# The end of a ReLU row-sum kernel: GpSimd alone waits for the stores and clears the semaphores

## Chip, cores and metric

The kernel runs on one core of one Trainium2 chip. The metric is device microseconds of one execution. Times in traces are microseconds from the start of the span, which is the first of the program's own instructions (SyncE's first load); ns are marked.

## The reference

```python
x = randn(32, 512, 1024)  # float32, 64 MiB
out = np.sum(np.maximum(x, 0), axis=-1)  # 32 x 512, float32
```

16,384 rows of 1,024 numbers are clamped at zero and summed. The data are read once, and the output is 64 KB.

## The kernel before

The body is written by hand with its own semaphores. Its last part and the closing block are what matters here. Three stores, all issued by SyncE, each add 16 to a semaphore `stored`; the last one writes two columns of the result, 1 KB.

```python
def tile_relu_sum_kernel(tc, x, out):
    nc = tc.nc
    sems = Semaphores(tc)
    tc.close()
    tc.compile()
    nc.cur_bb = nc.bb_map[tc.start_bb_name]
    body = nc.cur_bb.bb.instructions
    ends = list(body)
    body.clear()
    n_stores = relu_sum(nc, sems, x, out)
    body.extend(ends)

    nc.cur_bb = nc.bb_map[tc.start_bb_name + "_end"]   # the closing block
    body = nc.cur_bb.bb.instructions
    ends = list(body)
    body.clear()
    nc.sync.wait_ge(sems.stored, 16 * n_stores)
    body.extend(ends)
    issue_ahead_of_the_barrier(tc, EARLY)
# ... cut ...
    def store(m, n, act, dve):
        nonlocal n_store
        dst, src = sums(m, n)
        nc.sync.wait_ge(sems.act, act)
        nc.sync.dma_start(out=dst, in_=src).wait_op(sems.dve, dve, "sem-ge").then_inc(
            sems.stored, 16
        )
        n_store += 1
# ... cut: loads, clamps, sums ...
    store(NT - 2, 2, n_act, n_dve)
    return n_store
```

The closing block (`ends`) that the framework makes holds, in this order: a drain on SyncE; a barrier of all five engines; on GpSimd a drain and one instruction that clears the range of the kernel's semaphores; a second barrier of all engines. A barrier is a drain that adds to a gather semaphore and a wait for a release semaphore on four engines, and on GpSimd a drain, a wait for four arrivals and a release. (A drain names no tile in the trace; here it carries a wait for a semaphore or an increment of one, or neither. A release is the increment that lets the waiting engines go on.)

Of the kernel before, what the change touches and what calls it, by code (L numbers as in the profile page):

```python
# [23 lines left out]
def kernel(tc: tile.TileContext, x: bass.AP, out: bass.AP):  # L24
# [9 lines that stand above are left out]
    n_stores = relu_sum(nc, sems, x, out)  # L34
    body.extend(ends)

    nc.cur_bb = nc.bb_map[tc.start_bb_name + "_end"]
    body = nc.cur_bb.bb.instructions
    ends = list(body)
    body.clear()  # L40
    nc.sync.wait_ge(sems.stored, 16 * n_stores)
    body.extend(ends)
    issue_ahead_of_the_barrier(tc, EARLY)


# [169 lines left out]
    return n_store  # L215


def issue_ahead_of_the_barrier(tc: tile.TileContext, n_loads: int):


    SP = mybir.EngineType.SP
    blocks = tc.nc.main_func.blocks
    opening = blocks[0].instructions
    body = next(b for b in blocks if b.name == tc.start_bb_name).instructions
    loads = [i for i in body if i.engine == SP][:n_loads]
    for i in loads:
        assert isinstance(i, mybir.InstDMACopy)
        body.remove(i)
    at = next(
        n  # L230
        for n, i in enumerate(opening)
        if i.engine == SP and isinstance(i, mybir.InstDrain)
    )
    opening[at:at] = loads
# [30 lines left out]
```

## Time and profile before

| | before |
|---|---|
| time, median | 163.16 us (163.13 to 163.45, 3 runs) |
| span of the program's own instructions | 160.70 us |
| share of the DMA engines' span taken by loads and stores | 97.6% |
| VectorE, ScalarE busy | 73%, 64% |
| last increment of `stored` | 159.90 us |
| time minus span | 2.44 us |

From the page of the kernel before, the span, the busy times (microseconds, share of the span, instructions) and the DMA queue (packets, megabytes, share of 16 engines' span):

```profile
span 160.7 us, 162 instructions
...
DVE 117.0 (73%) x47; ACT 102.8 (64%) x52; POOL 0.2 (0%) x4
...
q1 hardware_dynamic: 2592, 67.18, 97.6%
```

The body is bound by reading HBM: the transfers fill 97.6% of the queue's span and the two compute engines wait for them. The end of the chain that ended last (start, length, what):

```profile
127.97 28.83 DMA piece<-in_x_dram
156.80 0.02 issue
156.82 1.20 DVE piece L136 x6
158.02 0.02 issue
158.04 0.44 DVE piece L204
158.48 0.01 DVEq L29
```

So arithmetic is over at 158.48 us, and 2.2 us of the span follow it. What SyncE waits for there (total, times, longest):

```profile
SPq L29 <- DMA out_dram<-res: 1.1, 1, 1.1
...
SPq L29 <- PEq L29: 0.6, 2, 0.4
```

Line 29 is that of all instructions that the framework made. They are listed in the view of that source line (durations least, median, most in ns; first and last start in us):

```profile
L29 POOLq EVENT_SEMAPHORE  x4: 17/17/17, 160.0 to 160.6; - x4
L29 POOLq DRAIN  x3: 34/41/82, 0.7 to 160.4; - x3
L29 SPq DRAIN  x3: 7/7/7, 159.9 to 160.2; - x3
L29 PEldq DRAIN  x2: 8/8/8, 0.9 to 160.3; - x2
L29 ACTq DRAIN  x2: 14/596/1177, 156.5 to 160.2; - x2
L29 DVEq DRAIN  x2: 19/236/452, 158.1 to 160.2; - x2
L29 SPq EVENT_SEMAPHORE  x2: 17/17/17, 160.1 to 160.6; - x2
L29 ACTq EVENT_SEMAPHORE  x2: 17/17/17, 160.1 to 160.6; - x2
L29 DVEq EVENT_SEMAPHORE  x2: 21/21/21, 160.1 to 160.6; - x2
L29 PEldq EVENT_SEMAPHORE  x2: 51/51/51, 160.1 to 160.7; - x2
L29 POOLq EVENT_SEMAPHORE_RANGE_CLEAR  x1: 136/136/136, 160.3 to 160.3; - x1
```

These are SyncE's wait, the two barriers and the clearing between them. Some first drains start early (TensorE's at 0.9 us, ScalarE's at 156.5), as these engines have nothing left to do; everything after the start of SyncE's waiting drain at 159.92 runs in the last 0.8 us. None of it counts as busy time, so the page's busy rows show nothing of this.

The program's span is not the end of the timed interval. Time minus span is 2.44 us, and the trace's semaphore events show what happens in it. These events stand in the trace itself, and no view of the profile prints them. Semaphore 2, which no instruction of the program names, is incremented nine times (I call this a walk, the time between two increments a hop, and the engine whose turn it is a station); semaphores 7 to 255 are updated, the last of them from 161.36 to 162.02 us, from the middle of this walk on; then comes a second walk of nine. I call this stretch the runtime's ending. That name, "sync-barrier semaphore" for semaphore 2 and "resets" for the updates are names only: the trace tells neither who makes these events nor what the updates write. A walk of the same nine increments stands ahead of the span, too: the eight hops of this opening walk took 371 ns.

| event, kernel before | us |
|---|---|
| last increment of `stored` | 159.901 |
| walk 1, increments 1, 2, 3 | 160.936, 160.970, 161.175 |
| walk 1, increment 9 | 161.460 |
| walk 2, increments 1, 2 | 162.248, 162.358 |
| walk 2, increment 9 | 162.682 |
| a DMA transfer of 8,192 bytes, start and end | 162.807 to 163.375 |

### The profile page before, as it was taken

The numbers are of one execution on the slowest core, as the hardware profiler recorded it, in microseconds if no ns is written. First come the engines' busy times: TensorE is split into PE (matmuls) and PEld (weight loads), VectorE is DVE, ScalarE is ACT, GpSimd is POOL, SyncE is SP. The second block draws the span as 40 slices with busy tenths as digits, with TensorE's granted clock in tenths as the row PEclk, the third lists the DMA queues.
The fourth block names the chain that finished last, engine by engine and source line by source line (L and its number), as shares of the span: only waits on it lengthen the run. The fifth ranks groups of instructions, "written<-read, shape, count | busy, mean of one in ns | idle before, by whom it ended". The sixth has DMA issues, their size and how long they took to land.

```text
span 160.7 us, 162 instructions
## 1 busy us (share of the span) xinstructions
DVE 117.0 (73%) x47; ACT 102.8 (64%) x52; POOL 0.2 (0%) x4
## 2 busy tenths in 40 slices
DVE  0000000009999499994999999999999999998984
ACT  3000059990799709995099932999249992696882
POOL 0000000000000000000000000000000000000000
DMA  7996996996996996996996996996996997998992
GB/s 261 522 522 261 522 522 261 522 522 261 522 522 261 522 522 261 522 506 277 522 489 294 522 489 294 522 489 294 522 489 294 522 440 343 392 481 371 424 389 47
DMA packets 2592, 67.18 MB, mean 418 GB/s; under 512 B 672, under 2 KB 1184, under 8 KB 1312
## 3 DMA queue, kind: packets, MB, share of 16 engines
q1 hardware_dynamic: 2592, 67.18, 97.6%
HBM read 67.11 MB, written 0.07 MB: 418 GB/s over the span
## 4 chain that ended last, share of the span: by engine, by line
DMA 43%; DVE 33%; ACT 17%; another core or an unknown queue 3%; SPq 1%; issue 0%; DVEq 0%
DVE res L119 32%; DMA io<-in_x_dram 25%; DMA piece<-in_x_dram 18%; ACT io L111 17%; SPq L93 1%; DVE piece L136 1%; DVE piece L204 0%; DVEq L29 0%
## 5 line engine op out<-in xcount | busy, mean ns | idle before, releaser
L119 DVE TENSOR_REDUCE res<-io 128x8 f32<-128x8192 f32 (+3 forms) x9 | 97.9, 10933 | 40.1 <-ACT io L111 40.1
L111 ACT ACTIVATE io<-io 128x8192 f32<-128x8192 f32 (+3 forms) x9 | 79.2, 8826 | 47.2 <-DMA io<-in_x_dram 47.2
L126 ACT ACTIVATE io<-io 128x1024 f32<-128x1024 f32 x21 | 21.9, 1044 | 6.8 <-DMA io<-in_x_dram 6.8
L136 DVE TENSOR_SCALAR_CACHE_REDUCE io<-io 128x1024 f32<-128x1024 f32 x15 | 17.4, 1215 | 0.9 <-DMA io<-in_x_dram 0.8
L126 ACT ACTIVATION_READ_ACCUMULATOR io<-io 128x1 f32 x21 | 3.9, 187 | 0.0
L111 ACT ACT_TABLE_LOAD x1 | 1.3, 1283 | 0.8 <-PEq L249 0.8
L136 DVE TENSOR_SCALAR_CACHE_REDUCE piece<-piece 128x244 f32<-128x244 f32 (+2 forms) x3 | 1.2, 416 | 0.4 <-DMA piece<-in_x_dram 0.4
L136 DVE DVE_READ_ACCUMULATOR io<-io 128x1 f32 x15 | 1.2, 82 | 0.0
L204 DVE TENSOR_SCALAR_CACHE_REDUCE piece<-piece 128x271 f32<-128x271 f32 x1 | 0.4, 436 | 0.0
L136 DVE DVE_READ_ACCUMULATOR piece<-piece 128x1 f32 x3 | 0.2, 82 | 0.0
L249 POOL MEMSET const-bfloat16-1.0<- 128x1 bf16 x1 | 0.1, 102 | 0.0
L249 POOL MEMSET const-uint8-127<- 128x1 uint8 x1 | 0.1, 101 | 0.0
L249 POOL MEMSET const-float32-0.0<- 128x1 f32 x1 | 0.1, 99 | 0.2 <-issue 0.2
L249 POOL MEMSET const-float32-1.0<- 128x1 f32 x1 | 0.1, 98 | 0.0
L204 DVE DVE_READ_ACCUMULATOR piece<-piece 128x1 f32 x1 | 0.1, 84 | 0.0
## 6 DMA issues: line engine op xcount, KB each, us to landing
io<-in_x_dram SPq DMA_DIRECT2D x1, 4096.0 KB, 21.6
io<-in_x_dram SPq DMA_DIRECT2D x1, 2048.0 KB, 26.1
io<-in_x_dram SPq DMA_DIRECT2D x1, 1024.0 KB, 28.1
io<-in_x_dram SPq DMA_DIRECT2D x1, 512.0 KB, 28.9
piece<-in_x_dram SPq DMA_DIRECT2D x1, 134.0 KB, 28.4
piece<-in_x_dram SPq DMA_DIRECT2D x1, 130.0 KB, 28.6
piece<-in_x_dram SPq DMA_DIRECT2D x1, 126.0 KB, 28.7
piece<-in_x_dram SPq DMA_DIRECT2D x1, 122.0 KB, 28.8
```

What stands on the lines that cost most here:

```text
L93: dma = nc.sync.dma_start(out=dst, in_=src)
L111: i = nc.scalar.activation(out=ap, in_=ap, func=RELU)
L119: nc.vector.tensor_reduce(out=res[:, m : m + n], in_=ap, axis=mybir.AxisListType.X, op=ADD).wait_op(sems.act, n_act, "sem-ge").then_inc(se ...
L126: i = nc.scalar.activation(out=ap, in_=ap, func=RELU, accum_out=res[:, m : m + 1])
L136: i = nc.vector.tensor_scalar(out=ap, in0=ap, scalar1=0.0, scalar2=None, op0=MAX, op1=ADD, accum_out=accum_out,)
L204: nc.vector.tensor_scalar(out=last[:, :], in0=last[:, :], scalar1=0.0, scalar2=None, op0=MAX, op1=ADD, accum_out=res[:, NT - 1 : NT],).wai ...
L249: nc = _bacc.Bacc("TRN2", target_bir_lowering=False, num_devices=1)
```

## The change

The intent is to take the two barriers and a hand-over between engines off the end of the kernel. Only GpSimd stays: it waits for the stores itself and clears, while the other four engines run through to the runtime's ending.

```diff
     nc.cur_bb = nc.bb_map[tc.start_bb_name + "_end"]
     body = nc.cur_bb.bb.instructions
-    ends = list(body)
+    clear = semaphore_clear(body)
     body.clear()
-    nc.sync.wait_ge(sems.stored, 16 * n_stores)
-    body.extend(ends)
+    nc.gpsimd.wait_ge(sems.stored, 16 * n_stores)
+    body.extend(clear)
     issue_ahead_of_the_barrier(tc, EARLY)
+
+def semaphore_clear(instructions):
+    pool = [i for i in instructions if i.engine == mybir.EngineType.Pool]
+    at = next(
+        n for n, i in enumerate(pool) if getattr(i, "is_reset_sema", False)
+    )
+    return pool[at : at + 2]
```

The change removes 4 closing instructions each from TensorE, ScalarE and VectorE, 5 from SyncE and 6 from GpSimd: 23 of the 162 that the page counts.

## The prediction

> What bounds the kernel now. The page gives a span of 160.7 us. The table of DMA queues has the loads at 97.6% of the 16 engines' span; VectorE is busy 73%, ScalarE 64%. The chain of waits ends with VectorE's last piece, at 158.48 us from the span's start. HBM reading bounds the body, and the change touches none of it: the listing of instructions shows the same work on every engine. Only the ending can move.
>
> The ending before, from the trace's closing block and its semaphore events (us from the span's start):
> - 158.51 SyncE issues the last store; its 16th increment lands at 159.90.
> - 159.92 SyncE's drain sees it. Barrier 1 runs to about 160.14.
> - 160.16 GpSimd's drain (82 ns), 160.27 range clear (136 ns).
> - Barrier 2: GpSimd's gather and release at 160.52 and 160.60; TensorE's last event ends the span at 160.70.
> - The runtime's ending: the sync-barrier semaphore gets nine increments, 160.94 to 161.46. The third comes 205 ns after the second (38 ns at the opening), at 161.175. [...]a second walk ends at 162.68, 0.48 us short of the timed 163.16.
>
> [...] I take the late third arrival for GpSimd: it steps slowest (about 79 ns between closing instructions), and its last instruction begins 579 ns before that increment. This is inferred; the trace doesn't name the incrementing engine.
>
> The change removes SyncE's waiting drain and 22 barrier instructions (two barriers: four engines with two each, GpSimd with three), and moves the wait to GpSimd's drain. Nothing new is executed; 162 instructions become about 139. The other engines reach the runtime's barrier early and wait there.
>
> Estimated ending after, from the durations above:
> - stores complete at 159.90; GpSimd's drain starts some 23 ns later (its lag on the gather semaphore), 159.92;
> - clear 111 ns later, 160.035, ending at 160.17: the span ends here, 0.53 us shorter;
> - GpSimd's next instruction 165 ns after the clear's start, 160.20. Before, it was about 79 ns after the last release, 160.675, and the third increment came 500 ns after that. So it now comes at 160.70 in place of 161.175.
>
> Gain: about 0.24 us before the clear and 0.24 us after it, together 0.47 us, all on the critical path, since nothing else lies between the last store and the end. The walk and resets only shift. That is 0.3% of the time.
>
> Predicted: 162.69 us, 8 times in 10 between 162.35 and 163.05. Faster by over 2%: 0.01; within 2%: 0.985; slower by over 2%: 0.005.
>
> What would show each step. The span falls to about 160.2 us. Of the closing block only a drain and a range clear on GpSimd remain, 110 ns apart, the drain 20 ns after the last store increment. Loads, busy times and the time of VectorE's last piece stay within 0.2 us. The third increment comes late again, about 0.8 us after the last store increment in place of 1.27, and the time falls nearly as much as the span.
>
> What would make it wrong. The timed interval could end apart from the runtime's walk: then the gain is the span's 0.53 us, or zero. GpSimd could wake slower from a DMA semaphore. The third increment could be another engine's, with fixed work not tied to GpSimd's last instruction: then less is saved. And timing varies by 0.3 us from run to run (163.13 to 163.45), nearly as much as the gain.

0.24 us before the clear and 0.24 us after it, from the durations in the trace of the kernel before (0.239 and 0.236 unrounded), came to 0.47 us, and 163.16 less 0.47 to 162.69 us.

## The result, and the profile after

| | before | after |
|---|---|---|
| time, median | 163.14 us (162.99 to 163.45, 4 runs) | 162.21 us (162.14 to 162.35, 4 runs) |
| ratio | | 0.9942 (95%: 0.9924 to 0.9959) |
| profiled execution | 163.14 us | 162.35 us |
| its span | 160.70 us | 160.24 us |
| its time minus span | 2.44 us | 2.11 us |

A ratio is the mean time of one kernel's runs over that of the other's in the same rounds, so not quite the ratio of the medians. The median fell by 0.93 us, about twice what was predicted, and lies below the predicted range. The profiled execution of the kernel after is the slowest of its four, so the two profiled executions differ by less, 0.79 us.

The same lines of the page after:

```profile
span 160.2 us, 139 instructions
...
DVE 116.9 (73%) x47; ACT 102.8 (64%) x52; POOL 0.2 (0%) x4
...
q1 hardware_dynamic: 2592, 67.18, 97.9%
```

The end of its chain, and all that is left of the framework's closing block (in the view of line 29):

```profile
128.06 28.80 DMA piece<-in_x_dram
156.87 0.02 issue
156.89 1.18 DVE piece L137 x6
158.07 0.02 issue
158.09 0.45 DVE piece L205 x2
```

```profile
L29 POOLq DRAIN  x1: 88/88/88, 160.0 to 160.0; - x1
L29 POOLq EVENT_SEMAPHORE_RANGE_CLEAR  x1: 136/136/136, 160.1 to 160.1; - x1
```

The body is as before: the last piece starts 0.05 us later (158.09 for 158.04). The barriers are gone, and SyncE has no wait on line 29 any more. The drain starts 24 ns after the last store increment (159.988 after 159.964; SyncE's, before, started 16 ns after it), the clearing 117 ns after the drain. The first two increments of walk 1 now come at 1.01 and 157.79 us, and the third at 160.77: the walk starts long before the stores are done and waits at its third station.

Where the time went, term by term, between the two profiled executions (all from semaphore events and the two times):

| stretch | before, us | after, us | difference, us | predicted, us |
|---|---|---|---|---|
| span start to last increment of `stored` | 159.901 | 159.964 | +0.063 | 0 |
| from there to walk 1, increment 3 | 1.274 | 0.803 | -0.471 | -0.47 |
| to walk 1, increment 9 | 0.285 | 0.285 | 0 | 0 |
| to walk 2, increment 1 | 0.788 | 0.829 | +0.041 | 0 |
| to walk 2, increment 9 | 0.434 | 0.358 | -0.076 | 0 |
| from there to the time's value | 0.458 | 0.111 | -0.347 | 0 |
| sum | 163.14 | 162.35 | -0.79 | -0.47 |

The predicted term came out as predicted. What was not predicted is mostly the last row: 0.35 us after the runtime's last walk. The last row takes the timed interval as starting with the span. A DMA transfer of 8,192 bytes of the kind `instruction` (I call such a transfer a fetch), from 162.807 to 163.375 us, after walk 2, is in the trace before and is not in the trace after.

### The profile page after: what moved, and what is told of

Read it like the earlier page. It is cut to its first block, busy times and chain, and to the rows that moved or that the text cites. A ratio compares the mean times of both kernels' runs of the same rounds, so it can differ in the third digit from the quotient of the medians.

```text
span 160.2 us, 139 instructions
## 1 busy us (share of the span) xinstructions
DVE 116.9 (73%) x47; ACT 102.8 (64%) x52; POOL 0.2 (0%) x4
## 4 chain that ended last, share of the span: by engine, by line
DMA 43%; DVE 33%; ACT 17%; another core or an unknown queue 3%; SPq 1%; issue 0%
DVE res L120 32%; DMA io<-in_x_dram 25%; DMA piece<-in_x_dram 18%; ACT io L112 17%; SPq L94 1%; DVE piece L137 1%; DVE piece L205 0%
```

## The experiments

Theory A, at first: the 0.35 us hang on how many instructions some engine has, as the fetch after walk 2 stands in the trace of the kernel with 162 instructions and not in that of the kernel with 139. By what means a count would move a fetch was an assumption of mine that no run shows. Whether a count moves it, and whose, is what the runs test. Rival B: it is the barriers, as they make the other engines reach the runtime's ending late. Later a sharper theory, H, replaced A.

All kernels of this section gave correct results. "Time minus span" needs no comparison between executions whose loads land a little earlier or later, so it is the finer measure. It compares only kernels whose span ends with the same instruction, though: from the end of the span to the third increment it is 0.47 us in the kernel before (TensorE's last event ends the span) and 0.53 us after the change (GpSimd's clearing does), and the kernels without clearing end with SyncE's wait. Walk numbers are of the profiled execution. The runs came in four batches on three chips, each with its own runs of the kernel before (medians 162.92, 162.95, 163.16 and 163.06 us).

| run | time, us | ratio to before (95%) | last `stored` to walk 1 incr. 3 | time minus span | walk 2, hop 1, ns | fetch after walk 2 |
|---|---|---|---|---|---|---|
| before | 163.14 | | 1.274 | 2.44 | 110 | yes |
| after | 162.21 | 0.9942 (0.9924 to 0.9959) | 0.803 | 2.11 | 34 | no |
| e1_second_barrier_kept | 162.42 | 0.9967 (0.9953 to 0.9982) | 1.041 | 2.00 | 34 | no |
| e2_first_barrier_kept | 162.37 | 0.9963 (0.9948 to 0.9978) | 1.037 | 2.05 | 34 | no |
| e3_counts_restored | 162.54 | 0.9971 (0.9954 to 0.9989) | 0.797 | 2.50 | 123 | yes |
| e4_sync_waits_no_clear | 161.39 | 0.9905 (0.9890 to 0.9920) | before it | 1.57 | 34 | no |
| e5_fill_tensor | 162.21 | 0.9955 (0.9940 to 0.9970) | 0.803 | 2.07 | 35 | no |
| e6_fill_scalar | 162.04 | 0.9949 (0.9931 to 0.9968) | 0.804 | 1.94 | 85 | no |
| e7_fill_vector | 162.22 | 0.9961 (0.9945 to 0.9978) | 0.804 | 2.16 | 34 | no |
| e8_fill_sync | 162.32 | 0.9958 (0.9943 to 0.9973) | 0.803 | 2.11 | 34 | no |
| e9_fill_gpsimd | 162.34 | 0.9960 (0.9935 to 0.9984) | 0.797 | 2.12 | 35 | no |
| e10_before_gpsimd_12 | 163.07 | 0.9994 (0.9980 to 1.0008) | 1.274 | 2.27 | 131 | yes |
| e11_no_clear_scalar_8 | 161.28 | 0.9882 (0.9867 to 0.9897) | before it | 1.35 | 35 | no |
| e12_fill_scalar_8 | 162.17 | 0.9939 (0.9927 to 0.9952) | 0.803 | 1.89 | 35 | no |
| f1_fill_scalar_vector | 162.47 | 0.9964 (0.9941 to 0.9988) | 0.803 | 2.44 | 83 | yes |
| f2_all_but_scalar | 162.25 | 0.9945 (0.9927 to 0.9964) | 0.798 | 2.11 | 34 | no |
| f3_all_but_vector | 162.14 | 0.9942 (0.9921 to 0.9964) | 0.797 | 1.94 | 130 | no |
| f4_before_scalar_vector_4 | 162.53 | 0.9962 (0.9943 to 0.9981) | 1.275 | 1.92 | 34 | no |

### One barrier at a time

The first two runs undo half of the change each. In the first, GpSimd waits and clears and the second barrier stays; in the second, SyncE waits and the first barrier stays.

```diff
-    clear = semaphore_clear(body)
+    ends = list(body)
+    at = next(n for n, i in enumerate(ends) if getattr(i, "is_reset_sema", False))
     body.clear()
     nc.gpsimd.wait_ge(sems.stored, 16 * n_stores)
-    body.extend(clear)
+    body.extend(ends[at:])
```

The other has `nc.sync.wait_ge(...)` and `body.extend(ends[: at + 2])`.

> Only SyncE's wait and barrier 1 are gone; GpSimd waits, clears, then barrier 2. From the last store increment to the third increment of the runtime's first walk: 1.27 us in the kernel before, 0.80 after the change; my sum gives 1.04 here. Theory A (instruction counts: the unexplained 0.35 us at the very end, after the second walk, hangs on how many instructions some engine has): here each engine has half of the removed instructions back, so the 0.35 is there or gone as a whole: 162.9 or 162.5 us. Theory B (late arrival: the 0.35 is there when the four other engines reach the runtime's ending late, just before GpSimd): they are late here, so 162.9 us, with time minus span 2.4.

> SyncE's wait and barrier 1 are kept, barrier 2 is gone. My sum: third increment 1.04 us after the last store increment. Theory A: as with the second barrier kept, same counts but for one on SyncE, so the same ending: 162.9 or 162.5 us. Theory B: the four engines leave barrier 1 some 0.15 us before GpSimd begins its drain, but are well ahead of GpSimd's arrival in the runtime; if it is lateness against GpSimd that counts, 162.5 us, time minus span 2.1.

Measured: 162.42 and 162.37 us, and 1.041 and 1.037 us from the last store increment to the third increment, where 1.04 was expected of both. So each barrier costs the same 0.24 us on GpSimd's path. Time minus span was 2.00 and 2.05 us, so the extra 0.35 us is gone in both. Rival B falls with the first of them: there the four engines are held by the second barrier, and the extra is gone all the same. A new detail: in both, the eighth increment of walk 2, on the way back, came 184 and 170 ns after the seventh, and 34 ns in the kernels before and after. (The 0.15 us in the second text are, in the trace of the kernel before, the time from SyncE's leaving barrier 1 at 160.124 us to GpSimd's clearing at 160.274; GpSimd's drain begins at 160.163, 0.04 us after SyncE leaves.)

### The counts restored

Idle drains are put in, as many on each engine as the change had removed, where they hold up nothing: early, and SyncE's five after its last store. Most later runs edit the numbers of the `fill` list below.

```diff
+    fill = [(nc.tensor, 4), (nc.scalar, 4), (nc.vector, 4), (nc.gpsimd, 6)]
+    for engine, n in fill:
+        for _ in range(n):
+            engine.drain()
     n_stores = relu_sum(nc, sems, x, out)
+    for _ in range(5):
+        nc.sync.drain()
```

> The changed kernel with as many idle drains put in early (SyncE's: after its last store) on each engine as the change removed there (TensorE 4, ScalarE 4, VectorE 4, GpSimd 6, SyncE 5). They do nothing and lie off the critical path. Theory A: the 0.35 us after the second walk comes back: about 162.55 us, time minus span 2.45, third increment still 0.80 us after the last store increment. Theory B: 162.2 us, time minus span 2.1.

Measured: 162.54 us; GpSimd's path as after the change (0.797 us), but time minus span 2.50, a fetch after walk 2, and 0.458 us from walk 2's end to the time, as before the change. The 0.35 us come back with 23 instructions that do nothing, 18 of them at the very start of the kernel. The view of their source line in this kernel (SyncE's are on another) shows where they ran:

```profile
L37 POOLq DRAIN  x6: 34/34/41, 0.7 to 1.1; - x6
L37 ACTq DRAIN  x4: 8/8/8, 0.8 to 0.9; - x4
L37 DVEq DRAIN  x4: 10/10/10, 0.8 to 0.9; - x4
L37 PEldq DRAIN  x4: 8/8/8, 0.9 to 1.1; - x4
```

### No clearing at all

```diff
     body.clear()
-    nc.gpsimd.wait_ge(sems.stored, 16 * n_stores)
-    body.extend(clear)
+    nc.sync.wait_ge(sems.stored, 16 * n_stores)
```

> No barriers and no clearing; SyncE alone waits for the stores (the trace shows the runtime updating semaphores 7 to 255 in its own ending). GpSimd's slow steps leave the critical path, so no late third increment; SyncE, last of the walk up, arrives instead, an estimated 0.35 us after the last store increment (its steps take about 55 ns against GpSimd's 79). My sum: 0.5 us less than the changed kernel: 161.7 us. Theory A: the same 2.1 or less from the end of GpSimd's part, no 0.35 back; theory B likewise. If semaphores had to be cleared by the program, it would give wrong results or hang in the repeats.

Measured: 161.39 us. The first line of its page shows one instruction less than after the change:

```profile
span 160.0 us, 138 instructions
```

In this trace the walk waits at its stations, and the stations can be told apart: increment 1 came at 0.99 us (an engine with nothing to do), increment 2 at 157.73 (ScalarE's last work ended just before), increment 3 at 157.77, 39 ns later, increment 4 at 158.66 (just after VectorE's last sum) and increment 5 at 160.09, 0.145 us after the last store increment (159.944), which only SyncE waits for. Increment 1 is TensorE's: with early drains on TensorE alone (e5, below) it comes at 1.27 us in place of 1.01 after the change. So the third station, the one left over, is GpSimd, as the prediction had inferred: it is late only in kernels where GpSimd has something to wait for. The order is thus TensorE, ScalarE, GpSimd, VectorE, SyncE. The estimate of 0.35 us for SyncE was too long. The last store increment to the end of walk 1 is 0.309 us here, 1.088 us after the change.

### One engine at a time

In these texts, "the one" is the engine whose count brings the 0.35 us back; the block that the first speaks of is the fetch of 8,192 bytes after walk 2.

> The changed kernel with four idle drains on TensorE alone, early. Restoring all engines' counts brought 0.33 us back after the second walk, with a block of instructions being fetched there. Theory A1 (TensorE's stream is the one[...]): 162.55 us, time minus span 2.5, a fetch in the trace after the second walk. If it is another engine's: 162.2 us, time minus span 2.1, no fetch.

> Four idle drains on ScalarE alone. With its count as before, the second walk's first hop (to the walk's second engine, which I take for ScalarE) took 110 to 123 ns in place of 34; with half of it (one barrier kept), the hop back was 170 to 184 ns in place of 34. So theory A expects the first hop of the second walk at 110 to 123 ns here. If ScalarE's stream also ends the timed interval: 162.55 us and a fetch after the second walk; otherwise 162.2 to 162.3 us, time minus span about 2.15.

> Four idle drains on VectorE alone. If VectorE's stream is the one[...]: 162.55 us, time minus span 2.5, a fetch after the second walk. Otherwise 162.2 us, 2.1, no fetch. The first hop of the second walk stays at 34 ns.

> Five idle drains on SyncE alone, after its last store. If SyncE's stream is the one[...]: 162.55 us, time minus span 2.5, a fetch after the second walk. Otherwise 162.2 us, 2.1, no fetch.

> The changed kernel with six idle drains on GpSimd alone, early, so that its count alone is as before. None of the other four engines brought the 0.35 us back, so theory A leaves GpSimd: 162.55 us, time minus span 2.45, a fetch of instructions after the second walk, timed end 0.35 us later against the second walk's end than after the change. If none of it comes back, it takes several engines together, or A is wrong.

The edits are the `fill` above with one engine's entry kept (for SyncE, the loop). None of the five brought the 0.35 us back. SyncE and GpSimd did nothing: 2.11 and 2.12 us of time minus span for 2.11. TensorE took 0.04 us away (2.07), and that lies between the walks: from the end of walk 1 to walk 2 it is 0.785 to 0.788 us in the seven kernels in which TensorE has its four more (before, e3, e5, e10, f2, f3, f4) and 0.828 to 0.832 us in all others. This is the term of +0.041 in the table above. ScalarE took time away, and moved a delay: walk 2's first hop, into ScalarE's station, took 85 ns in place of 34 (110 to 123 had been expected), and time minus span was 1.94 us (about 2.15 expected). VectorE moved the timed end by 0.05 us against the end of walk 2 (0.158 us after it, against 0.111 to 0.119 with none, TensorE's, SyncE's or GpSimd's). I had expected GpSimd once the other four had failed. That was wrong.

> The kernel before with twelve more idle drains on GpSimd, early. Theory A: [...]more instructions, and yet 0.3 us faster than before, about 162.6 us, time minus span 2.1 in place of 2.4, no fetch after the second walk. If the barriers themselves cost the 0.35: no faster than before, 162.95 us.

This one, `(nc.gpsimd, 12)` in the kernel before, failed too: 163.07 us against 163.16, ratio 0.9994. The fetch after walk 2 stayed. It was shorter in the profiled execution (342 ns for 568), and the timed end came earlier with it: that is what led to theory H.

### ScalarE further on

> The version without clearing (161.39 us) with eight idle drains on ScalarE, early. Four of them took 0.2 us off the changed kernel[...]. Theory A: 161.15 us, time minus span 1.3, first hop of the second walk 34 ns. Otherwise 161.4 us.

> The changed kernel with eight idle drains on ScalarE, early. With four, the first hop of the second walk took 85 ns (34 with none) and the timed end came 0.22 us earlier against the second walk's end. Theory A: [...]first hop 34 ns, time 162.0 us, time minus span 1.9.

With eight instructions on ScalarE, walk 2's first hop was back at 35 ns, and time minus span was 1.35 us (1.57 without them) and 1.89 us (2.11 without). The medians, 161.28 and 162.17 us, moved less than I expected, and their intervals overlap those of the kernels without the eight, so the times alone don't show this gain; time minus span does, as all four runs of the first and all five of the second lie at 1.4 and 1.9 us.

Put in order of ScalarE's count, the delay travels through the runtime's ending:

| ScalarE instructions more than after the change | where its delay shows |
|---|---|
| 0 (after) | no hop late, but the time ends 0.23 us later against walk 2's end than with 8 |
| 2 (one barrier kept) | walk 2, on the way back: 170 to 184 ns in place of 34 |
| 4 (before, e3, e6, e10, f1, f3) | walk 2, on the way in: 83 to 131 ns in place of 34 |
| 8, barriers gone (e11, e12) | nowhere |
| 8, barriers kept (f4, below) | walk 1, on the way in: 175 ns in place of 34 |

The more instructions ScalarE has, the earlier in the ending the delay comes. That the place of the delay goes with ScalarE's count is shown; why it does is not. One more record ties it to a fetch: with eight on ScalarE a fetch of 8,192 bytes stands in the trace 0.63 us after ScalarE's increment of walk 1 (158.63 to 159.39 us in e12, 158.94 to 159.55 in e11), and in neither kernel without the eight is there one anywhere in the span or after it. I call it ScalarE's fetch, as ScalarE's count is all that differs.

### Theory H: ScalarE's fetch and VectorE's late end, together

If the timed interval is taken to begin not with the span but with GpSimd's first memset (0.23 us later in every trace), its end falls on the end of the recorded fetch: within 3 ns in the kernel before (163.372 and 163.375), in e3 (162.741 and 162.743) and in e10 (163.177 and 163.175). Theory H: ScalarE with its four extra instructions starts a fetch that runs on for 0.1 to 0.7 us after walk 2; the interval includes it only if another engine is still at work when it starts, and VectorE's four extra instructions make VectorE that engine. That an engine still at work keeps the interval open is an assumption: no record names what ends it.

> The changed kernel with four idle drains on ScalarE and four on VectorE. Theory H: with four more instructions [...]its fetch runs about 0.1 to 0.7 us after the walk's end; with four more VectorE ends at 0.39 us after it (0.12 without), late enough that this fetch still falls into the timed interval, which then ends with it. So the two together bring the 0.35 us back: 162.5 us, time minus span 2.4, a fetch after the second walk. Rival R (three or more engines, or the sum of counts, are needed): 162.0 to 162.2 us, no fetch.

> All counts as before but ScalarE's (TensorE 4, VectorE 4, GpSimd 6, SyncE 5). Theory H: as with VectorE's four alone: 162.2 us, time minus span 2.15, no fetch after the second walk, first hop of the second walk 34 ns. If ScalarE is not needed: 162.55 us with a fetch.

> All counts as before but VectorE's (TensorE 4, ScalarE 4, GpSimd 6, SyncE 5). Theory H: as with ScalarE's four alone: 162.05 us, time minus span 1.95, no fetch in the timed interval, first hop of the second walk 85 to 123 ns. If VectorE is not needed: 162.55 us with a fetch.

Measured: with exactly these two filled, 162.47 us, time minus span 2.44, a fetch from 162.193 to 162.686 us, and the time's end, counted from the memset, at 162.691. With all but ScalarE's, 162.25 us and 2.11, no fetch, first hop 34 ns. With all but VectorE's, 162.14 us and 1.94, no fetch, first hop 130 ns. All three as theory H said. One of the four runs without VectorE's had a time minus span of 2.4 us; its trace was not kept, and I leave it open. The margin is thin: counted from the memset, the time ends 0.115 us after walk 2 here and 0.122 us in e6, and the fetch starts 0.125 to 0.384 us after it where it is recorded, so single executions on the other side are no surprise under H. With VectorE's four the time ends 0.384 to 0.389 us after walk 2 (f2, e7), just late enough for each of the recorded starts; that this is VectorE's own end, as the text of f1 has it, is the theory's assumption. R, the rival with three or more engines, falls.

> The kernel before, all barriers kept, with four more idle drains on ScalarE and four on VectorE, early. Theory H: [...]the fetch out of the end: time minus span 1.9 to 2.0 in place of 2.4, about 162.6 us although nothing is taken away. If the barriers themselves cost it: as before, 163.0 us.

The last run adds instructions to the kernel before, `(nc.scalar, 4), (nc.vector, 4)`, and keeps all barriers. Two lines of the view of line 29, and the view of the drains' line:

```profile
L29 PEldq EVENT_SEMAPHORE  x2: 51/51/51, 160.1 to 160.6; - x2
L29 POOLq EVENT_SEMAPHORE_RANGE_CLEAR  x1: 136/136/136, 160.3 to 160.3; - x1
```

```profile
L37 ACTq DRAIN  x4: 8/8/8, 0.8 to 0.9; - x4
L37 DVEq DRAIN  x4: 10/10/10, 0.8 to 0.9; - x4
```

The barriers run where they ran before, and the span is the same 160.7 us. Yet the time is 162.53 us against 163.06 in the same rounds (ratio 0.9962), with 1.92 us of time minus span in place of 2.44; all four runs show 1.9. The fetch is now at 161.763 to 162.218 us, ahead of walk 2's first increment (162.246), which it does not hold up. So the barriers had no part in the extra 0.35 us: instructions added at two engines take it away as well as instructions removed. VectorE's own delay seems to sit in walk 2's fourth increment now (179 ns for 44).

### The fastest version

The version without clearing and with eight idle drains on ScalarE ran at 161.28 us, ratio 0.9882 to the kernel before; without the drains it ran at 161.39 us, ratio 0.9905. Both beat the changed kernel's 0.9942. They leave the program's semaphores as they are and rely on the runtime's ending, in which semaphores 7 to 255 are updated (of the 249, the records of 22 and 23 are missing in the traces of these two versions, 115 among them, on which the kernel waits, and of 0 to 5 in the others; whether only the record is missing, and what an update writes, the traces don't tell). All their runs were correct. The drains are tuned to one stream length, so I would not keep them.

## Why the prediction was wrong

- The body was right: nothing in it moved but the landing of the loads by some hundredths of a microsecond.
- The waits on GpSimd's path were right. The third increment was predicted 0.80 us after the last store increment in place of 1.27; it came at 0.803. The runs with one barrier each gave 1.041 and 1.037, so the sum of 0.24 and 0.24 holds term by term. That the third station is GpSimd was an inference; the run without clearing showed it.
- The span was right: 160.24 us for "about 160.2 us".
- The step that failed is "The walk and resets only shift." It sized everything after walk 1 at no change. Measured between the profiled executions, this rest changed by -0.38 us: -0.076 in walk 2, -0.347 after it, +0.041 between the walks.
- What stood in its place: the change also shortened the instruction streams. Four instructions less on ScalarE and on VectorE took ScalarE's fetch out of the timed end and its delay out of walk 2's first hop (110 ns before, 34 after). Filling exactly these two streams again brought time minus span from 2.11 to 2.44 us; of the other three, filled one at a time, only TensorE's moved it, by the 0.04 us between the walks and the other way. Of the 0.79 us between the profiled executions (0.93 between the medians), then, 0.47 belong to the waits that the change meant to remove, and 0.38 to the runtime's ending, which the fills move; loads that landed 0.06 us later took some of it back.
- The warning that the timed interval "could end apart from the runtime's walk" was near it, but I drew the wrong bound from it. The fetch at 162.8 to 163.4 us was in the trace of before and could have been asked about.
- The range of 0.7 us was sized by the scatter between runs and left no room for a wrong term.

What stays open: the rule by which the timed interval ends is inferred from four coincidences of 2 to 5 ns. Whether the core is truly free 0.35 us sooner, or only the counted interval is shorter, these runs don't tell. Time minus span of the kernel before scatters from 2.2 to 2.5 us; I take it for the fetch's length (307 to 568 ns where it is recorded after walk 2), or for its falling outside the interval in some executions, without having shown either.

## What to carry to other kernels

At the end of this kernel, what counted first was when the last engine reached the runtime's own ending, so leave only the last wait there, on an engine that gets there fast (here SyncE, whose step followed the last store by 0.145 us, against GpSimd's 0.803 with its clearing; the run moved the wait and dropped the clearing at once, so the share of each is not shown; after the change, 0.66 us lie between the start of GpSimd's range clear at 160.105 us and its step in the walk at 160.767). Here 0.33 us were no more than a different number of instructions in two streams (time minus span 2.11 us after the change, 2.44 with ScalarE's and VectorE's four put back): before believing a cause, restore the counts with idle instructions and see whether the gain stays. Compare time minus span, and not only the time, when loads scatter by as much as the effect.
